# Six reorderings of products and banks in a one-core decoder trunk: up products, a w_out tile, embedding banks, triangular products, a branch tile, first masks

## The chip, the cores and the metric

The kernel runs on one core of one Trainium2 chip. The metric is the device time of one execution in microseconds (us), as a median of runs.

## The reference

One layer of a decoder trunk on a stream x of 512 tokens and 1024 channels, in fp32. The parts that the change touches:

```python
# mixer: one input projection gives q, k, v of three token mixers and three gates
proj = x @ w_in
(da_q, da_k, da_v, sb_q, sb_k, sb_v, dl_q, dl_k, dl_v, gates) = split(proj)
# A differential attention (4 heads), C dilated attention (12 heads), and
# B stick-breaking attention (8 heads):
z = q @ k.T * scale
log_keep = where(before, log_sigmoid(-z), 0.0)
later = cumsum(log_keep, axis=3, reverse=True) - log_keep
a = where(before, exp(log_sigmoid(z) + later), 0.0)
o = a @ v
# each branch: o_i @ w_branch_i;  merged = sum_i sigmoid(gate_i) * branch_i
x = layer_norm(alpha * x + merged @ w_out)
# MLP with squared ReLU, 1024 -> 4096 -> 1024, and a gated embedding of 256 channels
x = layer_norm(alpha * x + relu(x @ w_up)**2 @ w_down + sigmoid(x @ w_g) * (p @ w_p))
```

## The kernel before, in words

**Products.** Every product of fp32 matrices is three products of split operands (`mm3`, lines 86 to 89): a rounded high part and a low remainder, high by high (L87), high by low (L88), low by high (L89). Each writes a bank of PSUM, 128 x 512 fp32.

**Weights.** Weights come in chunks of 128 x 1024. The SyncE queue loads a chunk into one of six raw slots (L211, L213). ACT (ScalarE) casts it to the high part (L243, `wh<-raw`) and DVE (VectorE) subtracts to the low part (L245, `wl<-raw,wh`). The pair lies in a ring of six slots, and a slot is free again when PE (TensorE) has run the last product on the chunk six places earlier. Sums of weight chunks for the seven-product scheme below are made in DRAM by transfers that GpSimd (POOL) issues.

**Order.** `trunk()` fills a list `items`. An item has chunks `c`, the code that issues its products `mm`, the code that reads the bank out `ev`, the chunks that it needs, and the function that gives it a bank. A loop (L1970 to L2053) walks the list: it waits until the chunks are split, issues the reading out of the previous item, steps the side generators (stick-breaking heads `sb_head`, dilated heads, blocks of the differential attention `da_block`), and issues the item's products. A list scheduler then orders the instructions of each engine by its own estimates; each engine runs its list in that order.

**Banks.** PSUM has eight banks in two rotating pools: `mm_bank` (L80, two banks) and `at_bank` (L83, six). An item takes a bank from the pool of two if it names none.

**Up projection.** The MLP's up product is done in eight column groups, here called layers 0 to 7 after `up_parts(m)` (L1159). Each runs a seven-product scheme on 2 x 2 blocks: operand "12" of the weights against one form of x, "11" against another, and sums of blocks (operands 0, 1, 2) against t6, t7 and others. It is done for two pairs of column halves, j = 0 and 1; each pair keeps one bank `x` of the pool of two, whose left half (HB) and right half (HC) are 256 wide. `part_a(j)` does the "12"-product (12 products of 256 columns) into HC, ACT copies HC out (L1195), then the "11"-product (12 products) goes into HB of the same bank, and DVE adds the two (L1201). Parts b, c and e follow. The first layers stand alone; from layer 1 on, parts of the down projection are put between (`mlp_items`, L1310).

**The other places.** `wout_items` multiplies the merged branches, turned by PE (`turn_item`: transposes L794, ACT cast L798, DVE L799), by w_out (L887 to L889), eight steps k per tile of 128 tokens. `ple_items` multiplies the embedding by w_p (L955 to L960, copy L961). `first_branch` multiplies branch outputs by w_branch (L690 to L692), beside blocks of the differential attention, which turn rotary columns on DVE (L101). `t_item` makes transposed q and k tiles (mm3, then L101) and yields to the side generators once in its loop over k. `sb_head` sums log_keep over keys by products with a triangular matrix (`tri_r`, L1666) for four key blocks kb; blocks 3 and 2 share one bank of 512 columns, 256 each.

Of the kernel before, what the change touches and what calls it, by code (L numbers as in the profile page):

```python
# [55 lines left out]
def trunk(tc, a, out):  # L56
    nc = tc.nc
    es = ExitStack()
    with es:
# [14 lines left out]
        def slot(name, dt=F32):  # L74
            return big.tile([P, 512], dt, name=nm(name), tag="s", bufs=NSLOT)
# [190 lines left out]
        def item(cs, mm, ev, need=None, bank=None, size=1.0):  # L266
            items.append({"c": cs, "mm": mm, "ev": ev, "need": need, "bank": bank, "size": size})
# [24 lines left out]
        def t_item(nt, name, j):  # L292
            w = a["wt"][nt - 2]
            cs = [chunk(w.rearrange("p k m -> p (k m)"), 1024)]
            k0 = 1 if nt < 4 else 0

            def mm(ps):
                c = cs[0]
                for k in range(k0, 8):
                    s = slice(k * P, k * P + P)  # L300
                    mm3(ps, c["h"][:, s], c["l"][:, s], xh[k], xl[k], k == 0, k == 7)
                    if k == 3:
                        yield

            item(cs, mm, t_evac(name, j), bank=(lambda: begun[nt - 2]) if k0 else None)
# [55 lines left out]
        HB = slice(0, 256)  # L361
# [318 lines left out]
        def first_branch():  # L680
            for half in range(2):
                cs = [chunk(a["wb"][half, c].rearrange("p k n -> p (k n)"), 1024) for c in range(2)]
                for tt in range(4):
                    def mm(ps, tt=tt, cs=cs):
                        q = slice(tt * P, tt * P + P)
                        for k in range(4):
                            c = cs[k // 2]
                            n = slice(k % 2 * 512, k % 2 * 512 + 512)
                            h, lo = oTs[4 + k]
                            nc.tensor.matmul(ps, h[:, q], c["h"][:, n], start=k == 0, stop=False)  # L690
                            nc.tensor.matmul(ps, h[:, q], c["l"][:, n], start=False, stop=False)
                            nc.tensor.matmul(ps, lo[:, q], c["h"][:, n], start=False, stop=k == 3)  # L692

                    def ev(ps, tt=tt, half=half):
                        t = slot("b1")
                        e = nc.scalar.copy(t, ps)
                        marks.append(getattr(e, "ins", e))
                        merged[tt, half] = t
                    item(cs if tt == 3 else [], mm, ev, need=cs, size=0.5)
                    items[-1]["rate"] = 2.4  # L700

        bsum = {i: [dram.tile([P, 1024], F32, name=f"bsum{i}_{j}") for j in range(4)] for i in (0, 2)}
# [174 lines left out]
        def wout_items():  # L877
            for half in range(2):
                cs = [chunk(a["wo"][half, c].rearrange("p k n -> p (k n)"), 1024) for c in range(4)]
                for tt in range(4):  # L880
                    def mm(ps, tt=tt, cs=cs):
                        for k in range(8):
                            c = cs[k // 2]
                            s = slice((k % 2) * 512, (k % 2) * 512 + 512)
                            h, lo = merged_T[k // 4, tt // 2, k % 4 // 2]
                            q = slice(k % 2 * 256 + tt % 2 * P, k % 2 * 256 + tt % 2 * P + P)
                            nc.tensor.matmul(ps, h[:, q], c["h"][:, s], start=k == 0, stop=False)  # L887
                            nc.tensor.matmul(ps, h[:, q], c["l"][:, s], start=False, stop=False)
                            nc.tensor.matmul(ps, lo[:, q], c["h"][:, s], start=False, stop=k == 7)  # L889

                    def ev(ps, tt=tt, half=half):
                        y = xn.pop((tt, half))
                        if not half:
                            x1sum[tt] = small("lsm", 2)
                        i = nc.vector.scalar_tensor_tensor(y, y, ALPHA, ps, op0=OP.mult, op1=OP.add,
                                                           accum_out=x1sum[tt][:, half:half + 1])
                        st["added"] = getattr(i, "ins", i)
                        x1[tt, half] = y
                        if half:
                            pending.append(ln1_gen(tt))  # L900
                    item(cs if tt == 3 else [], mm, ev, need=cs, bank=at_bank)
                    for t in {0: [(1, 1, 0), (1, 1, 1)], 1: [(0, 1, 0), (0, 1, 1)]}.get(tt, ()) if not half else ():
                        turn_item(*t)
# [41 lines left out]
        def ple_items():  # L945
            cs = [chunk(a["wp"][half].rearrange("p k n -> p (k n)"), 1024) for half in range(2)]
            for half in range(2):
                for tt in range(4):
                    def mm(ps, tt=tt, half=half):
                        c = cs[half]  # L950
                        for k in range(2):
                            s = slice(k * 512, k * 512 + 512)
                            q = slice(tt * P, tt * P + P)
                            h, lo = pTs[k]
                            nc.tensor.matmul(ps, h[:, q], c["h"][:, s], start=k == 0, stop=False)  # L955
                            nc.tensor.matmul(ps, h[:, q], c["l"][:, s], start=False, stop=False)
                            nc.tensor.matmul(ps, lo[:, q], c["h"][:, s], start=False, stop=k == 1)

                    def ev(ps, tt=tt, half=half):
                        t = slot("ple")  # L960
                        nc.scalar.copy(t, ps)  # L961
                        ple[tt, half] = t
                    item([cs[half]] if tt == 3 else [], mm, ev, need=cs, bank=at_bank)


        sums_first = set()
# [192 lines left out]
        def up_parts(m):  # L1159

            cs = {}
            wu = a["wu"][m]

            def operand(n):
# [3 lines left out]

            def pair(j):
                js = slice(256 * j, 256 * j + 256)  # L1170
                b = {}

                def prod(ps, p, n, start, stop):
                    c = cs[n]
                    for k in range(4):
                        s = slice(512 * j + k * P, 512 * j + k * P + P)
                        mm3(ps, c["h"][:, s], c["l"][:, s], *forms[p][k], start and k == 0, stop and k == 3)
# [7 lines left out]
                def add(need, mm, ev, bank):  # L1185
                    if j == 0:
                        for n in need:
                            operand(n)
                    item([cs[n] for n in need] if j else [], mm, ev, need=[cs[n] for n in need], bank=bank)

                def part_a():
                    def mm(ps):
                        prod(ps[:, HC], 2, "12", True, True)
                        b["s"] = slot("up")
                        nc.scalar.copy(b["s"][:, HB], ps[:, HC])  # L1195
                        prod(ps[:, HB], 1, "11", True, False)

                    def ev(ps):
                        if j == 0:
                            hid[m] = [slot("hid") for _ in range(4)]  # L1200
                        nc.vector.tensor_add(hid[m][0][:, js], ps[:, HB], b["s"][:, HB])  # L1201
                    add(("12", "11"), mm, ev, bank("x", mm_bank))

                def part_b():
                    def mm(ps):
# [403 lines left out]
        def sb_head(hd):  # L1609
# [51 lines left out]
                yield  # L1661
            ah, al = {}, {}
            for kb, bi, c0, n in reversed(blk):
                ps = bank[bi][:, c0:c0 + n]
                for hl in (sph, spl):
                    nc.tensor.matmul(ps, tri_r, hl[bi][:, c0:c0 + n], start=False, stop=False, skip_group_check=True)  # L1666
                if kb < 3:
                    n2, hl = later[kb]
                    for t in hl:
                        nc.tensor.matmul(bank[bi][:, c0 + n - n2:c0 + n], ones_r, t, start=False, stop=False,  # L1670
                                         skip_group_check=True)
                if kb == 3:
                    continue
                n = w[bi]
                e = slot("a")[:, :n]
                nc.scalar.activation(e, bank[bi][:, :n], AF.Exp)
                h = slot("ah", F32R)[:, :n]
                lo = slot("al", F32R)[:, :n]
                nc.vector.tensor_copy(h, e)
                nc.vector.tensor_sub(lo, e, h.bitcast(F32))  # L1680
                ah[bi], al[bi] = h, lo
                if kb != 1:
                    yield
# [474 lines left out]
```

## Time and profile before

| | |
|---|---|
| runs shown | 1039.53, 1039.94, 1040.59 us; median 1039.94 |
| profiled execution | 1040.08 us, span 1038.1 us |
| granted clock of TensorE | 0.998 |
| PE busy | 1028.0 us (99%) |
| weight loads | 881.2 us (85%), beside PE |
| DVE busy | 787.0 us (76%) |
| ACT busy | 591.7 us (57%) |
| POOL busy | 180.1 us (17%) |

A row of the timeline has the start, the busy time, the engine, line and operation, and in brackets the engine's idle time just before it and what released it. PE's products are pipelined, so their busy times overlap; what one costs is read from the distance of its start to the next. PEld is the load of a product's stationary operand.

### The profile page before, as it was taken

The numbers are of one execution on the slowest core, as the hardware profiler recorded it, in microseconds if no ns is written. First come the engines' busy times: TensorE is split into PE (matmuls) and PEld (weight loads), VectorE is DVE, ScalarE is ACT, GpSimd is POOL, SyncE is SP. The second block draws the span as 40 slices with busy tenths as digits, with TensorE's granted clock in tenths as the row PEclk, the third lists the DMA queues.
The fourth block names the chain that finished last, engine by engine and source line by source line (L and its number), as shares of the span: only waits on it lengthen the run. The fifth ranks groups of instructions, "written<-read, shape, count | busy, mean of one in ns | idle before, by whom it ended". The sixth has DMA issues, their size and how long they took to land.

```text
span 1038.1 us, 15050 instructions
## 1 busy us (share of the span) xinstructions
PE 1028.0 (99%) x5448; PEld 881.2 (85%) x5448; DVE 787.0 (76%) x1412; ACT 591.7 (57%) x1010; POOL 180.1 (17%) x271
## 2 busy tenths in 40 slices
PE   9999999999999999999999999999999999999997
PEld 6888888889888888888888888889999889889886
DVE  6888667769765657779688885798768877877965
ACT  7566544536434645676675743775666556555651
POOL 0002411120211232411011040111111111111001
PEclk9999999999999999999999999999999999999999
DMA  8449968485976999977789795579999999998612
GB/s 309 121 156 271 277 193 217 120 290 144 285 182 222 271 272 294 238 205 199 227 269 235 267 320 182 160 222 319 331 290 315 301 306 340 303 295 279 235 57 81
DMA packets 71322, 249.21 MB, mean 240 GB/s; under 512 B 8808, under 2 KB 9592, under 8 KB 71248
## 3 DMA queue, kind: packets, MB, share of 16 engines
q0 software_dynamic: 32464, 116.21, 44.8%
q1 hardware_dynamic: 38208, 131.13, 35.1%
q8 instruction: 43, 0.70, 0.3%
q10 hardware_dynamic: 576, 0.92, 0.2%
q14 instruction: 31, 0.25, 0.1%
HBM read 246.10 MB, written 98.59 MB: 332 GB/s over the span
## 4 chain that ended last, share of the span: by engine, by line
PE 94%; DVE 2%; ACT 1%; DMA 1%; issue 1%; SPq 0%; POOL 0%; DVEq 0%; ACTq 0%; POOLq 0%
PE mm L87 10%; PE mm L88 10%; PE mm L89 10%; PE at L1261 4%; PE at L1262 4%; PE at L1263 4%; PE at L599 3%; PE at L600 3%; PE at L601 3%; PE mm L496 2%; PE mm L498 2%; PE mm L497 2%; PE at L89 1%; PE at L88 1%; PE at L87 1%; PE at L761 1%
## 5 line engine op out<-in xcount | busy, mean ns | idle before, releaser
L243 ACT CAST wh<-raw 128x1024 fp32r<-128x1024 f32 x257 | 268.6, 1049 | 242.0 <-PE mm L88 134.2
L245 DVE TENSOR_TENSOR wl<-raw,wh 128x1024 fp32r<-128x1024 f32 x257 | 312.7, 1223 | 112.9 <-ACT wh L243 111.3
L87 PE MATMUL mm<-xhT,wh 128*128 128x512 f32 x302 | 119.1, 394 | 0.0
L89 PE MATMUL mm<-xhT,wl 128*128 128x512 f32 x302 | 118.2, 391 | 0.0
L88 PE MATMUL mm<-xlT,wh 128*128 128x512 f32 x302 | 118.1, 391 | 0.0
L1261 PE MATMUL at<-wh,hh 128*128 128x512 f32 x188 | 73.7, 392 | 0.0
L87 PE MATMUL mm<-x1hT,wh 128*128 128x256 f32 x256 | 73.7, 288 | 0.0
L1262 PE MATMUL at<-wl,hh 128*128 128x512 f32 x188 | 73.7, 392 | 0.0
L1263 PE MATMUL at<-wh,hl 128*128 128x512 f32 x188 | 73.1, 389 | 0.0
L88 PE MATMUL mm<-x1lT,wh 128*128 128x256 f32 x256 | 72.2, 283 | 0.0
L89 PE MATMUL mm<-x1hT,wl 128*128 128x256 f32 x256 | 71.8, 283 | 0.0
L89 PEld LDWEIGHTS mm<-xhT,wl 128*128 128x128 f32 x302 | 56.8, 188 | 11.9
L87 PEld LDWEIGHTS mm<-xhT,wh 128*128 128x128 f32 x302 | 56.7, 188 | 11.0
L88 PEld LDWEIGHTS mm<-xlT,wh 128*128 128x128 f32 x302 | 56.7, 188 | 10.8
L87 PEld LDWEIGHTS mm<-x1hT,wh 128*128 128x128 f32 x256 | 48.7, 190 | 4.8 <-ACT up L1195 3.0
L88 PEld LDWEIGHTS mm<-x1lT,wh 128*128 128x128 f32 x256 | 48.8, 191 | 1.5
L89 PEld LDWEIGHTS mm<-x1hT,wl 128*128 128x128 f32 x256 | 48.6, 191 | 0.0
L1095 POOL DMA_DIRECT2D usum<-in_wu_dram x32 | 28.3, 921 | 101.6 <-DMA usum<-usum 34.8
L1095 POOL DMA_DIRECT2D dsum<-in_wd_dram x28 | 25.6, 936 | 102.5 <-DMA dsum<-dsum 37.0
L1263 PEld LDWEIGHTS at<-wh,hl 128*128 128x128 f32 x188 | 35.3, 188 | 7.7
L1261 PEld LDWEIGHTS at<-wh,hh 128*128 128x128 f32 x188 | 35.5, 189 | 6.0
L1262 PEld LDWEIGHTS at<-wl,hh 128*128 128x128 f32 x188 | 35.5, 189 | 5.5
(601 smaller groups left out, 2677.2 us busy)
## 6 DMA issues: line engine op xcount, KB each, us to landing
usum<-in_wu_dram POOLq DMA_DIRECT2D x48, 512.0 KB, 9.0
dsum<-in_wd_dram POOLq DMA_DIRECT2D x42, 512.0 KB, 8.9
raw<-in_wt_dram SPq DMA_DIRECT2D x38, 512.0 KB, 5.1
raw<-usum SPq DMA_DIRECT2D x32, 512.0 KB, 7.7
raw<-dsum SPq DMA_DIRECT2D x28, 512.0 KB, 7.0
raw<-in_wd_dram SPq DMA_DIRECT2D x25, 512.0 KB, 6.1
raw<-in_wu_dram SPq DMA_DIRECT2D x24, 512.0 KB, 7.6
raw<-in_wv_dram SPq DMA_DIRECT2D x18, 512.0 KB, 5.7
```

The source lines that it names most:

```text
L87: nc.tensor.matmul(ps, wh, xh, start=start, stop=False, skip_group_check=True)
L88: nc.tensor.matmul(ps, wh, xl, start=False, stop=False, skip_group_check=True)
L89: nc.tensor.matmul(ps, wl, xh, start=False, stop=stop, skip_group_check=True)
L243: i = nc.scalar.copy(h, raw)
L245: i = nc.vector.tensor_sub(lo, raw, h.bitcast(F32))
L599: nc.tensor.matmul(ps, h[:, q], c["h"][:, n], start=go, stop=False, skip_group_check=True)
L600: nc.tensor.matmul(ps, h[:, q], c["l"][:, n], start=False, stop=False, skip_group_check=True)
L601: nc.tensor.matmul(ps, lo[:, q], c["h"][:, n], start=False, stop=end, skip_group_check=True)
L1095: i = nc.gpsimd.dma_start(o, i, accum_op=OP.add, max_dma_last_dim=4096)
L1261: nc.tensor.matmul(ps, h[:, q], c["h"][:, s], start=go, stop=False, skip_group_check=True)
L1262: nc.tensor.matmul(ps, h[:, q], c["l"][:, s], start=False, stop=False, skip_group_check=True)
L1263: nc.tensor.matmul(ps, lo[:, q], c["h"][:, s], start=False, stop=end, skip_group_check=True)
```

## The change

1. Up products: `part_a(0)` does the "12"-products of both pairs, each into its own bank with its own copy; `part_a(1)` does the "11"-products of both, and issues pair 0's add (`first(0)`) between them. The chunk "11" is asked for with `part_a(1)`, so that in layers with down parts one down chunk is loaded ahead of it.
2. The third w_out tile (tt = 2, half 0) runs its steps k in the order 4 to 7, 0 to 3.
3. Embedding tiles 1 and 3 of half 0 take a bank of the pool of two.
4. For kb = 3 and 2 the triangular products of 256 columns become one of 512 for the high and one for the low part.
5. The branch tile tt = 1 of half 0 takes a bank of the pool of six.
6. `t_item` for nt = 2 yields after k = 4 instead of 3.

```diff
-                    if k == 3:
+                    if k == (4 if nt == 2 else 3):
                         yield
...
-                    item(cs if tt == 3 else [], mm, ev, need=cs, size=0.5)
+                    item(cs if tt == 3 else [], mm, ev, need=cs, size=0.5,
+                         bank=at_bank if tt == 1 and not half else None)
...
-                    def mm(ps, tt=tt, cs=cs):
-                        for k in range(8):
+                    ks = (4, 5, 6, 7, 0, 1, 2, 3) if tt == 2 and not half else range(8)
+
+                    def mm(ps, tt=tt, cs=cs, ks=ks):
+                        for k in ks:
...
-                    item([cs[half]] if tt == 3 else [], mm, ev, need=cs, bank=at_bank)
+                    item([cs[half]] if tt == 3 else [], mm, ev, need=cs,
+                         bank=None if tt % 2 and not half else at_bank)
...
                 def part_a():
+                    def first(i):
+                        nc.vector.tensor_add(hid[m][0][:, 256 * i:256 * i + 256], both[i]["x"][:, HB],
+                                             both[i]["s"][:, HB])
+
                     def mm(ps):
-                        prod(ps[:, HC], 2, "12", True, True)
-                        b["s"] = slot("up")
-                        nc.scalar.copy(b["s"][:, HB], ps[:, HC])
-                        prod(ps[:, HB], 1, "11", True, False)
+                        for i in range(2):
+                            if j == 0:
+                                if i:
+                                    both[i]["x"] = mm_bank()
+                                x, k = both[i]["x"], "12"
+                                prod(x[:, HC], 2, k, True, True, i)
+                                both[i]["s"] = slot("up")
+                                nc.scalar.copy(both[i]["s"][:, HB], x[:, HC])
+                            else:
+                                prod(both[i]["x"][:, HB], 1, "11", True, False, i)
+                                if not i:
+                                    first(i)
...
-                    add(("12", "11"), mm, ev, bank("x", mm_bank))
+                    operand(("12", "11")[j])
+                    need = [cs[("12", "11")[j]]]
+                    item(need, mm, ev, need=need, bank=(lambda: b["x"]) if j else bank("x", mm_bank))
...
-                ps = bank[bi][:, c0:c0 + n]
-                for hl in (sph, spl):
-                    nc.tensor.matmul(ps, tri_r, hl[bi][:, c0:c0 + n], start=False, stop=False, skip_group_check=True)
+                for hl in (sph, spl) if kb != 2 else ():
+                    nc.tensor.matmul(bank[bi][:, :w[bi]], tri_r, hl[bi], start=False, stop=False,
+                                     skip_group_check=True)
```

**Up products on PE, layer 0.** Before: the first product of each run of products, and the waits that it has. `mm_1497` is pair 0's bank, `mm_1503` pair 1's, `wh_1477` is chunk "12", `wh_1480` chunk "11", `wh_1483` and `wh_1486` the next operands; each run has 12 products but where the other pair cuts it in two (4 and 8, or 11 and 1).

```order
L87 MATMUL mm_1497_6921<-x1hT_6343,wh_1477_6820 128x256 [waits Activation_49]
...
L87 MATMUL mm_1503_6955<-x1hT_6343,wh_1477_6820 128x256
...
L87 MATMUL mm_1497_6921<-x1hT_6343,wh_1480_6826 128x256 [waits Activation_49]
...
L88 MATMUL mm_1503_6955<-x1lT_6344,wh_1477_6820 128x256
...
L89 MATMUL at_1511_6996<-t7h_1431_6602,wl_1484_6866 128x256 [waits DVE_49]
...
L87 MATMUL mm_1503_6955<-x1hT_6343,wh_1480_6826 128x256 [waits Activation_49]
...
L87 MATMUL mm_1497_6921<-t6h_1443_6642,wh_1486_6871 128x256 [waits DVE_49]
```

Now, with pair 1's bank named `mm_1499`:

```order
L87 MATMUL mm_1497_6905<-x1hT_6327,wh_1477_6804 128x256 [waits Activation_49]
...
L87 MATMUL mm_1499_6920<-x1hT_6327,wh_1477_6804 128x256
...
L87 MATMUL mm_1497_6905<-x1hT_6327,wh_1480_6810 128x256 [waits Activation_49]
...
L87 MATMUL mm_1499_6920<-x1hT_6327,wh_1480_6810 128x256 [waits Activation_49]
...
L89 MATMUL at_1511_6980<-t7h_1431_6586,wl_1484_6850 128x256 [waits DVE_49]
...
L87 MATMUL mm_1497_6905<-t6h_1443_6626,wh_1486_6855 128x256 [waits DVE_49]
```

Pair 0's "11"-product stood 4 products behind its "12"-product and now stands 12 behind; pair 1's stood 11 behind and now stands 12 behind.

**The copies on ACT, layer 0.** Before: the two copies of the "12"-products (L1195), and what stands around them.

```order
L1195 COPY up_1498_6934<-mm_1497_6921 128x256 [waits PE_49]
L243 CAST wh_1505_6982<-raw_1479_6824 128x1024 [waits DMAHW6_49,PE_49,Activation_49]
L1195 COPY up_1504_6968<-mm_1503_6955 128x256 [waits PE_49]
L243 CAST wh_1508_6988<-raw_1482_6830 128x1024 [waits DMAHW7_49,PE_49,Activation_49]
L1211 COPY up_1498_6934<-at_1511_6996 128x256 [waits DVE_49,PE_49]
```

Now (the copies are on line 1209):

```order
L1209 COPY up_1498_6918<-mm_1497_6905 128x256 [waits PE_49]
L243 CAST wh_1501_6935<-raw_1479_6808 128x1024 [waits DMAHW6_49,PE_49,Activation_49]
L1209 COPY up_1500_6933<-mm_1499_6920 128x256 [waits PE_49]
L243 CAST wh_1508_6972<-raw_1482_6814 128x1024 [waits DMAHW7_49,PE_49,Activation_49]
L1253 ACTIVATE hid_1504_6941<-hid_1504_6941 128x512 [waits DVE_49]
```

A cast stands between the two copies in both. It takes the ring slot of the chunk six places back, which is `wh_1477`, chunk "12", in both; the same holds in the other layers.

**The embedding on PE.** Before: the first products of the embedding's tiles 1 to 3 of half 0, all in banks of the pool of six.

```order
L955 MATMUL at_1389_6448<-wh_1349_6217,pTh_1356_6255 128x512 [waits DVE_49,Activation_49]
...
L957 MATMUL at_1389_6448<-wh_1349_6217,pTl_1359_6260 128x512
L955 MATMUL at_1397_6469<-wh_1349_6217,pTh_1356_6255 128x512 [waits DVE_49,Activation_49]
...
L957 MATMUL at_1397_6469<-wh_1349_6217,pTl_1359_6260 128x512
L955 MATMUL at_1405_6490<-wh_1349_6217,pTh_1356_6255 128x512 [waits DVE_49]
```

Now:

```order
L958 MATMUL mm_1389_6432<-wh_1349_6201,pTh_1356_6239 128x512 [waits PE_49]
...
L960 MATMUL mm_1389_6432<-wh_1349_6201,pTl_1359_6240 128x512
L958 MATMUL at_1397_6453<-wh_1349_6201,pTh_1356_6239 128x512 [waits DVE_49,Activation_49]
...
L960 MATMUL at_1397_6453<-wh_1349_6201,pTl_1359_6240 128x512
L958 MATMUL mm_1405_6474<-wh_1349_6201,pTh_1356_6239 128x512
```

The order of the products is the same; tiles 1 and 3 no longer use up a bank of the pool of six, so the tiles behind them take banks that come two places earlier in its rotation.

More of the change, by code (lines that the diff above doesn't have):

```diff
@@ L886, in mm @@
                             q = slice(k % 2 * 256 + tt % 2 * P, k % 2 * 256 + tt % 2 * P + P)
-                            nc.tensor.matmul(ps, h[:, q], c["h"][:, s], start=k == 0, stop=False)
+                            nc.tensor.matmul(ps, h[:, q], c["h"][:, s], start=k == ks[0], stop=False)
                             nc.tensor.matmul(ps, h[:, q], c["l"][:, s], start=False, stop=False)
-                            nc.tensor.matmul(ps, lo[:, q], c["h"][:, s], start=False, stop=k == 7)
+                            nc.tensor.matmul(ps, lo[:, q], c["h"][:, s], start=False, stop=k == ks[-1])
                     def ev(ps, tt=tt, half=half):
@@ L1161, in up_parts @@
             cs = {}
+            both = [{}, {}]
             wu = a["wu"][m]
@@ L1170, in pair, with prod @@
                 js = slice(256 * j, 256 * j + 256)
-                b = {}
-                def prod(ps, p, n, start, stop):
+                b = both[j]
+                def prod(ps, p, n, start, stop, j=j):
                     c = cs[n]
@@ L1200, in ev @@
                             hid[m] = [slot("hid") for _ in range(4)]
-                        nc.vector.tensor_add(hid[m][0][:, js], ps[:, HB], b["s"][:, HB])
-                    add(("12", "11"), mm, ev, bank("x", mm_bank))
+                        else:
+                            first(1)
+                    operand(("12", "11")[j])
+                    need = [cs[("12", "11")[j]]]
+                    item(need, mm, ev, need=need, bank=(lambda: b["x"]) if j else bank("x", mm_bank))
                 def part_b():
```

## The prediction

> **What bounds the kernel now.** I read the page first, then the waits of the matrix engine, then the timeline around each place that the change touches.
>
> From the page: the span, the matrix engine's busy time, the transfers by slice, and the chain that ended last.
>
> ```profile
> span 1038.1 us, 15050 instructions
> PE 1028.0 (99%) x5448; PEld 881.2 (85%) x5448; DVE 787.0 (76%) x1412; ACT 591.7 (57%) x1010; POOL 180.1 (17%) x271
> ...
> DMA  8449968485976999977789795579999999998612
> ...
> PE 94%; DVE 2%; ACT 1%; DMA 1%; issue 1%; SPq 0%; POOL 0%; DVEq 0%; ACTq 0%; POOLq 0%
> ```
>
> PE is busy 99% and carries 94% of the chain. Nothing can be gained except products or PE's own waits. The change removes 16 products and otherwise reorders, so its worth is the waits it takes away less the waits it makes. The weight loads (PEld) show them, with total us, times and longest:
>
> ```profile
> PEld mm L87 <- ACT up L1195: 3.0, 13, 0.3
> ...
> PEld mm L690 <- PE at L147: 0.7, 1, 0.7
> PEld at L955 <- ACT ple L961: 0.6, 1, 0.6
> ...
> PEld at L887 <- ACT mh L798: 0.5, 1, 0.5
> ```
>
> Four of the six edits stand in this list: the up copies (13 waits), the branch tile (L690), the embedding (L955) and the w_out tile (L887).
>
> **Up products: the first copy.** Layer 0 on PE and ACT:
>
> ```profile
> 709.69 0.39 PE L1017 MATMUL at<-wh,x1hT 128*128 128x512 f32 x1
> 709.92 0.39 PE L1018 MATMUL at<-wl,x1hT 128*128 128x512 f32 x1
> ...
> 712.17 0.70 PE L87 MATMUL mm<-x1hT,wh 128*128 128x256 f32 x2
> 712.70 0.28 PE L88 MATMUL mm<-x1lT,wh 128*128 128x256 f32 x1
> ...
> 714.73 0.28 PE L88 MATMUL mm<-x1lT,wh 128*128 128x256 f32 x1
> 714.85 0.28 PE L89 MATMUL mm<-x1hT,wl 128*128 128x256 f32 x1
> ...
> 716.17 0.28 PE L88 MATMUL at<-t7l,wh 128*128 128x256 f32 x1
> 716.46 0.39 PE L87 MATMUL mm<-x1hT,wh 128*128 128x256 f32 x1
> 716.68 0.28 PE L88 MATMUL mm<-x1lT,wh 128*128 128x256 f32 x1
> ...
> 712.06 0.36 ACT L1195 COPY up<-mm 128x256 f32<-128x256 f32 x1
> ...
> 715.09 1.05 ACT L243 CAST wh<-raw 128x1024 fp32r<-128x1024 f32 x1 [2.67 <-issue]
> 716.04 0.37 ACT L1195 COPY up<-mm 128x256 f32<-128x256 f32 x1
> ```
>
> A 256-wide product starts 0.12 us after the one before (714.73, 714.85), a 512-wide one 0.23. From 712.17 two steps take 0.53 instead of 0.24, so the first copy costs 0.29: PE had only 4 products of the other pair for cover. Half is the wait, the other 0.10 the next step, whose weight load wasn't ahead. In layer 2 the place is milder:
>
> ```profile
> 766.93 0.39 PE L1263 MATMUL at<-wh,hl 128*128 128x512 f32 x1
> 767.22 0.38 PE L87 MATMUL mm<-x1hT,wh 128*128 128x256 f32 x1
> 767.44 0.28 PE L88 MATMUL mm<-x1lT,wh 128*128 128x256 f32 x1
> ```
>
> Here it is 0.06 (0.29 against 0.23) and 0.10. Eight layers lie between: 8 x 0.16 = 1.3 us, which I take; 8 x 0.29 = 2.3 would be the upper end, though the row of 3.0 for all 13 waits leaves 1.8 beside the second places below. After the change 12 products (1.44 us) stand between. In layer 0 the last product that the first copy waits for started four steps ahead of 712.17, at 711.69; thirteen steps on is 713.25, and the copy ended at 712.42, so it would be 0.8 early: **−1.3**.
>
> **Up products: the second copy.** It is not the same case. In the order, ACT has a weight cast between the two copies of each layer, before and after, and the cast waits for the ring slot of chunk "12", which PE frees with the last 12-product, the very product that the second copy waits for. Layer 0 shows what that makes: last product starts 714.85, cast 715.09, copy 716.04, and PE goes on at 716.46, 1.61 us after 714.85. With 11 products for cover it wanted to go on at 716.29: 0.17, and 0.10 in the next step. Layer 1 has the same with the cast released by PE:
>
> ```profile
> 735.81 1.05 ACT L243 CAST wh<-raw 128x1024 fp32r<-128x1024 f32 x1 [1.73 <-PE mm L88]
> 736.77 0.37 ACT L1195 COPY up<-mm 128x256 f32<-128x256 f32 x1
> ...
> 736.93 0.28 PE L88 MATMUL at<-t7l,wh 128*128 128x256 f32 x1
> 737.19 0.38 PE L87 MATMUL mm<-x1hT,wh 128*128 128x256 f32 x1
> ```
>
> 0.14 and 0.10. Layers 0, 1, 3, 5 and 7 have it, together 0.27 + 4 x 0.24 = 1.23. After the change the cast still stands ahead of the copy, and 12 products cover instead of 11. One product more is 0.12: it leaves 0.05 in layer 0, 0.02 in the others, and the 0.10 each, 0.63 in all: **−0.6**. In layers 2, 4 and 6 a down chunk's 6 or 12 products also stand between; no wait there. If the copy passed the cast, all 1.23 would go; that is the upper end, and zero the lower.
>
> [...]
>
> New waits here: the first add is now issued between the two 11-products, and the 6-product of its bank follows 24 products (2.9 us) later instead of 36. On the vector engine a split (L245) of the delayed cast stands ahead of it, so it ends about 2.9 us after 714.85's counterpart; the 6-product wants the bank 36 steps, 4.4 us, after it. Cover remains: 0. The chunk "11" is loaded after a down chunk in layers with downs; see the rivals.
>
> **Branch, w_out, embedding.**
>
> ```profile
> 426.30 0.69 DVE L101 SCALAR_TENSOR_TENSOR da_klb<-mm,da_kb 64x512 fp32r<-64x512 f32 x1
> ...
> 427.14 0.47 PE L690 MATMUL mm<-wh,oTh 128*128 128x512 f32 x1 [0.32 <-DVE da_klb L101]
> ...
> 619.05 0.59 ACT L798 CAST mh<-mm 128x512 fp32r<-128x512 f32 x1 [1.24 <-PE mm L794]
> ...
> 624.47 0.50 PE L887 MATMUL at<-wh,mh 128*128 128x512 f32 x1 [0.24 <-ACT mh L798]
> ...
> 664.28 0.56 ACT L961 COPY ple<-at 128x512 f32<-128x512 f32 x1
> ...
> 664.90 0.50 PE L955 MATMUL at<-wh,pTh 128*128 128x512 f32 x1 [0.21 <-ACT ple L961]
> ```
>
> The branch tile waits for a pool-of-two bank that L101 reads until 426.99. In the pool of six it gets a bank free long before; the later tiles shift by one bank, still free in time. It lies between 0.32 (PE idle) and 0.7 (PEld): **−0.5**. The w_out tile waits for halves that were turned just ahead; the order now puts 12 products on halves cast at 619.05 first, 12 x 0.23 = 2.7 us of cover. Between 0.24 and 0.5, plus the next step: **−0.5**. The embedding tile waits for a bank whose copy ran 664.28 to 664.84; with two tiles in the pool of two it takes one emptied earlier. Between 0.21 and 0.6: **−0.5**.
>
> **Triangular products.** 32 products of 256 become 16 of 512 (the first row counts half of them, the high ones):
>
> ```profile
> L1666 PE MATMUL at<-sph,tri_r x32: 278/310/398, 29.9 to 217.9; 128*128 128x256 f32 x16, 128*128 128x384 f32 x8, 128*128 128x512 f32 x8
> ```
>
> 2 x 0.12 − 0.23 = 0.01 each: **−0.2**, between 0 and 0.3. [...]
>
> **First masks.**
>
> ```profile
> 20.26 0.69 DVE L101 SCALAR_TENSOR_TENSOR sb_k<-at,sb_k 64x512 fp32r<-64x512 f32 x1
> ...
> 21.09 0.53 PE L146 MATMUL at<-sb_q,sb_k 128*128 128x256 f32 x2 [0.36 <-ACT wh L243]
> ...
> 30.49 0.69 DVE L101 SCALAR_TENSOR_TENSOR sb_qlb<-mm,sb_qb 64x512 fp32r<-64x512 f32 x1
> ...
> 31.33 0.47 PE L496 MATMUL mm<-wh,xhT 128*128 128x512 f32 x1
> ```
>
> Three products (0.68) go ahead of the masks and hide their 0.36. But at 31.33 PE waits for a bank that L101 reads until 31.18, at the end of a row of vector and scalar work that PE doesn't drive. PE comes there earlier and waits longer: **0**, at best −0.5.
>
> **Sum.** 1.3 + 0.6 + 0.5 + 0.5 + 0.5 + 0.2 = 3.6 us. The profiled execution took 1040.08 us (2.0 outside its span), 0.14 above the median of 1039.94. 1039.94 − 3.6 = 1036.3; I write 1036.4. A difference of 0.2%, 2.1 us, is about what a measurement of this kernel can tell from none.
>
> **Rivals.**
>
> 1. Everything pays: the second copies too (0.6), the masks (0.5) and the first copies up to 1.8 (0.5): −5.2, 1034.7. Against it: the cast's place in the order. Chance 0.10.
> 2. Part comes back: the three single waits (1.5) were standing in for the chains of layer norm and gates behind them, and PE waits there instead: −2.1, 1037.8; with half of Up −1.2, 1038.7. For it: the masks are such a case. Against: no wait of PE on layer norm is in the list. Chance 0.28, of which 0.16 is still below the 0.2%, 0.12 within it.
> 3. Slower: a late chunk. From 712 us on the transfers are at 0.9 or more, and a down chunk is now loaded ahead of "11". If a cast between the copies waits for its data, the second copy stands behind it, and PE behind that: per layer one microsecond for each that the chunk is late, beyond the slack. The slack is what casts now wait for PE:
>
> ```profile
> ACT wh L243 <- PE mm L88: 70.6, 26, 4.1
> ```
>
> 2.7 us in the mean. It decides where a chunk comes over 2.7 us later than now; one more microsecond in eight layers gives 8 − 3.6 = +4.4, 1044.3. Chance 0.10.
>
> **Numbers.** The forecast has 0.52. Faster by over 0.2%: 0.52 + 0.10 + 0.16 = 0.78; within: 0.12; slower: 0.10. The range takes in the bounds of the terms and the second rival, 1034.9 to 1038.7; what it leaves out is mostly the third.
>
> **What the next profile would show.** Right: the row of L87 on the up copy falls from 13 waits to five of about 0.1; the rows of L690, L955 and L887 vanish from the list; the wait at 31.33 grows by about 0.5. Wrong: PE waiting for a cast or for data in the up layers, second places with more than 0.2 each, or a new wait on layer norm after the embedding.

## The result and the profile after

The changed kernel took 1037.52 us in the median of 9 runs (1036.55 to 1038.24), beside 1040.39 of the kernel before (9 runs, 1039.53 to 1040.92). The ratio is 0.9973, with a 95% interval of 0.9964 to 0.9982: 2.8 us faster by that ratio, where 3.6 were forecast. The profiled execution took 1037.48 us.

The page of the changed kernel:

```profile
span 1035.5 us, 15013 instructions
PE 1025.9 (99%) x5432; PEld 880.2 (85%) x5432; DVE 786.4 (76%) x1412; ACT 592.9 (57%) x1010; POOL 180.5 (17%) x271
...
DMA  8349968495976999977889896479999999999512
...
PE 91%; issue 4%; DVE 2%; DMA 1%; ACT 1%; POOL 0%; DVEq 0%; POOLq 0%; ACTq 0%
```

PE has 16 products fewer and is as full as before. The waits of the weight loads, from the same list as before:

```profile
PEld at L762 <- DVE b L773: 0.7, 2, 0.5
...
PEld mm L496 <- issue: 0.6, 1, 0.6
...
PEld at L1709 <- DVE sb_v L509: 0.4, 1, 0.4
...
PEld at L1021 <- ACT x1r L940: 0.2, 1, 0.2
```

All four rows that the forecast spoke of (the up copies, L690, L955, L887) are gone; what is left at the up copies is too short for the list and shows on the timeline. So is the masks' own row (L146 behind a cast, 0.5). In its place L496 has come, the wait at 31 us that was forecast for the masks. L1709 and L1021 are new, and L762 had one wait of 0.2 before (then L761); these three were not forecast. (Rows of L347, behind `wh` and `wl`, which also differ, 1.0 and 0.2 before and 1.2 and 0.8 now, belong to the first 31 us, where PE waits for its first chunks.) The timeline of PE at the places of the forecast, in the order up copy of layer 1, branch, w_out, embedding, masks:

```profile
734.63 0.28 PE L89 MATMUL mm<-x1hT,wl 128*128 128x256 f32 x1
734.76 0.38 PE L87 MATMUL mm<-x1hT,wh 128*128 128x256 f32 x1
734.98 0.28 PE L88 MATMUL mm<-x1lT,wh 128*128 128x256 f32 x1
...
427.00 0.39 PE L147 MATMUL at<-da_klb,da_qb 128*128 128x512 f32 x1
427.23 0.39 PE L690 MATMUL at<-wh,oTh 128*128 128x512 f32 x1
...
624.40 0.48 PE L890 MATMUL at<-wh,mh 128*128 128x512 f32 x1
624.71 0.40 PE L891 MATMUL at<-wl,mh 128*128 128x512 f32 x1
...
664.17 0.39 PE L960 MATMUL mm<-wh,pTl 128*128 128x512 f32 x1
664.39 0.39 PE L958 MATMUL at<-wh,pTh 128*128 128x512 f32 x1
...
31.37 0.47 PE L496 MATMUL mm<-wh,xhT 128*128 128x512 f32 x1 [0.41 <-DVE sb_qlb L101]
```

The branch and the embedding tile start one step (0.23 or 0.22) after the product before them. The w_out tile keeps 0.08 (0.31 to the next start instead of 0.23) of the 0.55 that the waiting product and the step behind it had before. The up copy keeps what the cast ahead of it leaves: 0.13 to 734.76 and 0.22 to 734.98, so 0.01 of waiting and 0.10 in the next step. ACT shows the cast and the copy of that place in the order that the forecast had read:

```profile
733.39 1.05 ACT L243 CAST wh<-raw 128x1024 fp32r<-128x1024 f32 x1
734.34 0.37 ACT L1209 COPY up<-mm 128x256 f32<-128x256 f32 x1
```

The masks' gain is back at 31.37, where PE now idles 0.41. The three waits that were not forecast, and what stands ahead of the last on ACT:

```profile
61.84 0.39 PE L88 MATMUL mm<-xlT,wh 128*128 128x512 f32 x1
62.24 0.38 PE L1709 MATMUL at<-ah,sb_v 128*128 128x256 f32 x1
62.46 0.28 PE L1711 MATMUL at<-al,sb_v 128*64 128x256 f32 x1
...
555.01 0.39 PE L600 MATMUL at<-wl,xhT 128*128 128x512 f32 x1
555.52 0.50 PE L762 MATMUL at<-wh,oTh 128*128 128x512 f32 x1
555.86 0.39 PE L763 MATMUL at<-wl,oTh 128*128 128x512 f32 x1
...
671.31 0.49 PE L927 MATMUL at<-ident,xn 128*128 128x128 f32 x3
671.80 0.50 PE L1021 MATMUL at<-wh,x1hT 128*128 128x512 f32 x1
672.14 0.39 PE L1022 MATMUL at<-wl,x1hT 128*128 128x512 f32 x1
...
671.10 0.65 ACT L940 COPY x1r<-at 128x256 f32<-128x256 f32 x2 [0.66 <-DVE x1lT L934]
```

Against undisturbed steps they cost 0.27 (62 us), 0.39 (555 us) and 0.27 (672 us, of which 0.09 was there before).

### The profile page after: what moved, and what is told of

Same layout as the page of the kernel before. It is cut to its first block, busy times and chain, and to the rows that moved or that the text cites. A ratio compares the mean times of both kernels' runs of the same rounds, so it can differ in the third digit from the quotient of the medians.

```text
span 1035.5 us, 15013 instructions
## 1 busy us (share of the span) xinstructions
PE 1025.9 (99%) x5432; PEld 880.2 (85%) x5432; DVE 786.4 (76%) x1412; ACT 592.9 (57%) x1010; POOL 180.5 (17%) x271
## 4 chain that ended last, share of the span: by engine, by line
PE 91%; issue 4%; DVE 2%; DMA 1%; ACT 1%; POOL 0%; DVEq 0%; POOLq 0%; ACTq 0%
PE mm L87 10%; PE mm L89 10%; PE mm L88 10%; PE at L1281 4%; PE at L1282 4%; PE at L1283 4%; PE mm L496 2%; PE mm L498 2%; PE mm L497 2%; PE at L601 2%; PE at L599 2%; PE at L600 2%; PE at L89 1%; PE at L88 1%; PE at L87 1%
## 5 line engine op out<-in xcount | busy, mean ns | idle before, releaser
L245 DVE TENSOR_TENSOR wl<-raw,wh 128x1024 fp32r<-128x1024 f32 x257 | 312.4, 1222 | 115.8 <-ACT wh L243 114.4
L87 PE MATMUL mm<-xhT,wh 128*128 128x512 f32 x302 | 119.1, 395 | 0.0
L87 PE MATMUL mm<-x1hT,wh 128*128 128x256 f32 x256 | 72.8, 284 | 0.0
L87 PEld LDWEIGHTS mm<-xhT,wh 128*128 128x128 f32 x302 | 56.7, 188 | 11.3 <-PE mm L498 0.2
L87 PEld LDWEIGHTS mm<-x1hT,wh 128*128 128x128 f32 x256 | 48.9, 191 | 1.9
```

Of the source, the lines that this page charges most:

```text
L87: nc.tensor.matmul(ps, wh, xh, start=start, stop=False, skip_group_check=True)
L245: i = nc.vector.tensor_sub(lo, raw, h.bitcast(F32))
```

## The experiments

Eight kernels were timed, five to eleven runs each, in five rounds beside runs of the kernel before. Where the text says "excess", it is the distance between two starts of PE less the usual one for that width, read from the timeline. "Pace" is the mean step from one product of 512 columns to the next of that width between 95 and 250 us, over the steps of 0.20 to 0.26 us. The "lead" of a run is how much earlier PE starts the same product than in the kernel before.

**Up products alone.** Edit 1 on the kernel before, nothing else (the whole edit stands in the change above).

```diff
 def part_a():
+    def first(i):
...
     def mm(ps):
-        prod(ps[:, HC], 2, "12", True, True)
...
+        for i in range(2):
...
```

> Edit 1 alone. Theory: the up stage gives what the trace of the whole change shows there, 13 waits on the up copy going to five steps of 0.10, about -1.9 to -2.0 us, and nothing is given back before or behind it, so the time is 1.9 us below before (ratio 0.9981). Rival: PE that is earlier in the up stage waits for casts or data later, so that the whole change's 2.8 us come mostly from the other edits: then this gives under 1 us.

Measured: 1037.67 us, ratio 0.9976 (0.9966 to 0.9986). PE leads by 0.27 us when the up stage begins (710 us) and by 2.48 at the end: the stage gives 2.2 us. The 0.27 is left of a lead of 0.4 from the first 31 us, where chunks arrive at other times from run to run (the casts that end ACT's first two waits for a DMA start at 4.39 and 6.64 us in before, at 4.22 and 7.03 in the change). The theory holds, at 2.2 rather than 1.9 us; the rival falls.

**Everything but the up products.**

Against the change (`up_parts` as before, edits 2 to 6 in place):

```diff
-                        for i in range(2):
-                            if j == 0:
...
+                        prod(ps[:, HC], 2, "12", True, True)
+                        b["s"] = slot("up")
+                        nc.scalar.copy(b["s"][:, HB], ps[:, HC])
+                        prod(ps[:, HB], 1, "11", True, False)
```

> Edits 2 to 6 without the up products. Theory: the branch's 0.5 is spent in a wait of about 0.4 near 555 us where PE waits for a bank whose reading stands behind a split of a chunk that comes late from DRAM, the masks' gain is spent at 31.3 us, and a wait of 0.27 near 62 us is new; what is left is w_out and the embedding, 0.9 less 0.3 at 672 us, so -0.6 to -0.9 us (ratio 0.9992). Rival: the waits at 62, 555 and 672 us are scatter of one execution; then -1.7 us (ratio 0.9984).

Measured: 1039.04 us, ratio 0.9989 (0.9980 to 0.9998). The five edits together give 1.1 us where the forecast had 1.7. The waits are there again: 0.25 at 61.8 us, 0.59 at 555 us, 0.27 at 671.7 us. In the profiled execution, one of the slower of the eleven (1039.70), PE's lead is 0.4 at 40 us and 0.4 at the end: there the gains and the waits cancel. The time (a gain of 0.2 to 2.1) does not tell the theory from its rival; the waits, there again, do. Of them the one at 555 us differs most between executions.

**The change a second time.** The same kernel, for a second profile and a second timing.

> The change as it is, a second profile. Theory: the waits at 62 us (0.27), 555 us (0.39) and 671.8 us (0.27) are there again within 0.1 each, and PE's start-to-start excess in the up stage is five times 0.10; time 2.8 us below before. Rival (scatter): at least two of the three differ by more than 0.2.

Measured: 1036.89 us, ratio 0.9967 (0.9955 to 0.9980). The waits at 62 us (0.26) and 672 us (0.26) are the same to 0.01. The one at 555 us is not there at all. The reading of PE's bank (L773, on DVE) stands behind the split of a chunk (L245), and the split waits for the cast of that chunk, which waits for its data from DRAM. Here the cast and the split in the change's first profile, then the cast in this one, where the split starts at 552.43 and waits for nothing:

```profile
551.96 1.05 ACT L243 CAST wh<-raw 128x1024 fp32r<-128x1024 f32 x1 [4.15 <-DMA raw<-in_wgm_dram]
553.04 1.23 DVE L245 TENSOR_TENSOR wl<-raw,wh 128x1024 fp32r<-128x1024 f32 x1 [0.42 <-ACT wh L243]
```

```profile
549.66 1.05 ACT L243 CAST wh<-raw 128x1024 fp32r<-128x1024 f32 x1 [1.96 <-DMA raw<-in_wgm_dram]
```

The same chunk, from the same place in the queue, came 2.3 us apart in two executions of one kernel. In the kernel before it came at 551.53 and PE just did not wait. So the wait at 555 us is scatter of a load that PE meets without slack; the other two belong to the kernel. It is not rare: of the six profiles with the branch edit four have it (0.30 to 0.59), of the six without it one (0.13). That the 0.5 us of the edit makes the difference is not shown: PE was due there at 555.24 in the change and at 555.27 in before. The theory holds for two of three.

**The second up copies on the vector engine.** Against the change:

```diff
-                                nc.scalar.copy(both[i]["s"][:, HB], x[:, HC])
+                                (nc.vector.tensor_copy if i else nc.scalar.copy)(both[i]["s"][:, HB], x[:, HC])
```

> The change, with the second copy of each layer made by the vector engine, where it stands ahead of the split of the chunk whose cast stands ahead of it on ACT. Theory (the cast ahead of the copy makes what is left): the five steps of 0.10 in layers 0, 1, 3, 5 and 7 vanish, 0.5 us faster than the change. Rival (what is left is the price of any first product on a bank that another engine has read, or the vector engine is as late): the five stay, time equal to the change within 0.2 us.

Measured: 1036.57 us, ratio 0.9969 (0.9957 to 0.9980), not to be told apart from the change by time (one of its six runs took 1040.02). By the profile, layer 1 has no step left, and the copy runs ahead of the split:

```profile
732.83 0.42 DVE L1209 COPY up<-mm 128x256 f32<-128x256 f32 x1 [0.24 <-PE mm L89]
733.79 1.23 DVE L245 TENSOR_TENSOR wl<-raw,wh 128x1024 fp32r<-128x1024 f32 x1 [0.54 <-ACT wh L243]
...
734.31 0.28 PE L89 MATMUL mm<-x1hT,wl 128*128 128x256 f32 x1
734.43 0.28 PE L87 MATMUL mm<-x1hT,wh 128*128 128x256 f32 x1
734.55 0.28 PE L88 MATMUL mm<-x1lT,wh 128*128 128x256 f32 x1
```

Layers 1, 3, 5 and 7 lose their 0.10; layer 0 gets 0.27 instead of 0.16, since there the copy stands behind other work of the vector engine (L991 from 712.63, the copy at 713.23). Net 0.3 us, not 0.5. That the cast ahead of the copy makes what was left is shown for four of five layers.

**First masks alone.** On the kernel before:

```diff
-                    if k == 3:
+                    if k == (4 if nt == 2 else 3):
```

> Edit 6 alone. Theory: its 0.5 us at 21 us come back in full as a wait of 0.56 at 31.3 us, and it makes the wait of 0.27 at 62 us; so 0.0 to +0.3 us against before (ratio 1.0000 to 1.0003). If also the pace of 512-wide products between 95 and 250 us is its doing, that reads 229.4 ns there instead of 228.8 (546 of them, +0.3 us), and the sum is +0.6. Rival: the wait at 62 us comes from the merged triangular products; then neither shows here.

Measured: 1040.20 us, ratio 1.0002 (0.9993 to 1.0011). No wait at 62 us, and the pace is 228.7 ns (538 steps), as before. The gain comes back ten microseconds later:

```profile
32.15 0.47 PE L496 MATMUL mm<-wh,xhT 128*128 128x512 f32 x1 [0.44 <-DVE sb_qlb L101]
```

So edit 6 is worth nothing, and the wait at 62 us is not its doing: the rival holds.

**Triangular products alone.** On the kernel before:

```diff
-                for hl in (sph, spl):
-                    nc.tensor.matmul(ps, tri_r, hl[bi][:, c0:c0 + n], start=False, stop=False, skip_group_check=True)
+                for hl in (sph, spl) if kb != 2 else ():
+                    nc.tensor.matmul(bank[bi][:, :w[bi]], tri_r, hl[bi], start=False, stop=False,
+                                     skip_group_check=True)
```

> Edit 4 alone. Theory: a pair of 256-wide products takes 236 ns there and one of 512 takes 233, so the 16 merges save 0.05 to 0.1 us in all, not 0.2; ratio 0.9999. If the slower pace of the other 512-wide products between 95 and 250 us (229.4 against 228.8 ns) comes with it, it costs 0.3 and the sum is +0.2 us. Rival: the pace is that of the masks' shift; then it reads 228.8 here.

Measured: 1040.72 us, ratio 1.0005 (0.9997 to 1.0014). The time alone does not settle the sign. The profile has the wait at 61.8 us (0.24) and the slower pace, 229.3 ns (547 steps). The merges themselves save 0.07 us per ten (between 95 and 260 us 20 products of 256 took 2.37 us in before, and ten of 512 take 2.30 in the change's second profile). So by the profile edit 4 costs 0.24 + 0.3 − 0.1, near +0.45 us; PE's lead falls from 0.41 at 40 us to nothing by 200 us.

**The four other edits.**

Against the change (edits 1, 2, 3 and 5 in place):

```diff
-                    if k == (4 if nt == 2 else 3):
+                    if k == 3:
...
-                for hl in (sph, spl) if kb != 2 else ():
+                for hl in (sph, spl):
```

> Edits 1, 2, 3 and 5, without masks and triangular products. Theory: no wait at 62 us, the pace between 95 and 250 us at 228.8 ns, the other gains as in the whole change, so 0.5 us faster than the change: 3.3 us below before (ratio 0.9968). Rival: those two edits carry their own weight; then this is equal to the change or slower by 0.2.

Measured: 1036.77 us, ratio 0.9965 (0.9953 to 0.9977). No wait at 62 us, pace 228.7 ns, span 1034.8 us beside 1035.5 and 1035.0 of the change. The mechanism is as the theory has it; by time it is not told apart from the change (0.9973 and 0.9967).

**The four, with copies of layers 1 to 7 on the vector engine.**

```diff
+                                (nc.vector.tensor_copy if i and m else nc.scalar.copy)(both[i]["s"][:, HB],
+                                                                                       x[:, HC])
```

> As the last, and with the second up copy of layers 1 to 7 on the vector engine. Theory: the 0.10 steps of layers 1, 3, 5 and 7 go as in the run with all second copies there, and layer 0 keeps its 0.10 instead of the 0.27 that it had there; so 0.4 us faster than the last (ratio 0.9964). Rival: what the vector engine's copy displaces there comes back as a wait; then no faster.

Measured: 1036.15 us, ratio 0.9961 (0.9949 to 0.9974), the fastest median of all, 3.9 us below before, though its interval overlaps those of the last and of the change. Layer 0 keeps its 0.16 and the other layers have none, as expected.

**Merged in heads 0 and 1 alone.** On the kernel before (an excerpt):

```diff
+                wide = hd < 2
+                cols = slice(0, w[bi]) if wide else slice(c0, c0 + n)
+                for hl in (sph, spl) if kb != 2 or not wide else ():
...
```

> Merged triangular products in heads 0 and 1 alone (4 merges of 16). These two move the order: on ACT a weight cast goes eight places forward, and on PE the first products of a later head's output go 13 forward. Theory (the order costs, not the merge): the wait of 0.24 to 0.27 at 62 us is there, and it alone or with the slower pace of 512-wide products between 95 and 250 us (229.4 ns). Rival (the merge itself slows the products beside it): pace 228.8 there, since no head after 70 us is merged.

**Merged in heads 2 to 7 alone.** The same, but for one line:

```diff
+                wide = hd >= 2
```

> Merged triangular products in heads 2 to 7 alone (12 of 16), which leaves the order at 62 us as before. Theory (the order costs): no wait at 62 us, and pace 228.8 between 95 and 250 us, so PE gains about 12 times 6 ns there. Rival (the merge itself slows the products beside it): no wait at 62 us, pace 229.4.

Both were profiled and run once: 1040.00 and 1040.02 us beside 1040.19 of before. The profiles split the two costs. With heads 0 and 1 merged the wait at 62 us is there (0.26) and the pace is 228.8; with heads 2 to 7 merged the wait is not there and the pace is 229.3. PE at 61 us in the first and in the second:

```profile
61.27 0.39 PE L88 MATMUL mm<-xlT,wh 128*128 128x512 f32 x1
61.66 0.39 PE L1691 MATMUL at<-ah,sb_v 128*128 128x256 f32 x1
```

```profile
60.95 0.40 PE L89 MATMUL mm<-xhT,wl 128*128 128x512 f32 x1
61.18 0.28 PE L1691 MATMUL at<-ah,sb_v 128*128 128x256 f32 x1
```

So the wait is the order's. With heads 0 and 1 merged the list scheduler puts four weight casts on ACT one or two places forward, the first two each ahead of a copy of `sb_v` (the expectation read this as one cast eight places forward). The vector engine's work behind them runs later, at its end the last subtraction for `sb_v` (L509), which starts at 61.18 instead of 61.00 and ends at 61.60, where PE wants it at 61.50. The pace comes with the merges of the later heads, so in that point the rival holds. Where it sits: behind the merged products and two of `ones_r`, PE is slower for ten products. From the kernel before, and then with heads 2 to 7 merged:

```profile
114.75 0.28 PE L1670 MATMUL at<-sph,ones_r 128*128 128x256 f32 x1
114.87 0.28 PE L1670 MATMUL at<-spl,ones_r 128*128 128x256 f32 x1
114.98 0.40 PE L87 MATMUL mm<-xhT,wh 128*128 128x512 f32 x1
...
117.26 0.39 PE L88 MATMUL mm<-xlT,wh 128*128 128x512 f32 x1
```

```profile
114.29 0.28 PE L1672 MATMUL at<-sph,ones_r 128*128 128x256 f32 x1
114.41 0.28 PE L1672 MATMUL at<-spl,ones_r 128*128 128x256 f32 x1
114.52 0.40 PE L87 MATMUL mm<-xhT,wh 128*128 128x512 f32 x1
...
116.85 0.39 PE L88 MATMUL mm<-xlT,wh 128*128 128x512 f32 x1
```

Ten steps from the first L87 take 2.28 us before and 2.33 after a merge, and so behind all five merges between 110 and 215 us. But slow steps are not the merge's alone. In the kernel before, ten steps behind products of 384 and 256 columns take 2.33 us too:

```profile
38.27 0.28 PE L1670 MATMUL at<-smp,ones_r 128*128 128x256 f32 x1
38.38 0.40 PE L496 MATMUL mm<-wh,xhT 128*128 128x512 f32 x1
...
40.72 0.39 PE L497 MATMUL mm<-wl,xhT 128*128 128x512 f32 x1
```

At 62 us ten steps take 2.31 in the kernel before, behind four triangular products of 256 columns, and 2.28 with heads 2 to 7 merged, where the order of the products there is the same as before. So neither the width of the triangular products nor the order alone fixes how long the ten steps take. What makes them slower the rows do not show; that stays open.

## Why the prediction was right, and where its terms were off

The sign and most of the mechanism were right; the sum was 0.8 us too large. By the time alone the forecast is not set apart from its second rival: 2.8 lies about midway between 3.6 and 2.1. The traces do that, term by term, and two terms were off in opposite directions:

- **Up products, −1.9 forecast: −2.2 measured** alone, from 710 us to the end. The second copies left what was forecast: five steps of 0.10, in layers 0, 1, 3, 5 and 7 and nowhere else, with 0.06 of waiting in layer 0 and 0.01 in the others, 0.63 in all. Reading the cast between the copies in the order, and its release by the very product that the copy waits for, was what made this term: with the copy on the other engine the steps of 0.10 went in four of the five layers. What the waits were before was misread. The place in layer 2 from which the forecast took 0.16 for each first copy is the second copy's:

```profile
762.15 0.35 ACT L1195 COPY up<-mm 128x256 f32<-128x256 f32 x1
766.80 0.37 ACT L1195 COPY up<-mm 128x256 f32<-128x256 f32 x1
...
762.42 0.40 PE L1262 MATMUL at<-wl,hh 128*128 128x512 f32 x1
762.66 0.28 PE L87 MATMUL mm<-x1hT,wh 128*128 128x256 f32 x1
```

The first copy ends at 762.50, and PE goes on at 762.66 without excess; the excess at 767.22 follows the second, which ends at 767.17. So "no wait there" was wrong for the second copies of layers 2, 4 and 6, which had 0.16 to 0.17 each. By the steps, the first copies cost 1.17 in seven layers and lost it all, near the 1.3 by luck, and the second fell from 1.73 to 0.63, by 1.1 instead of 0.6. That the list's 13 waits looked like eight first and five second copies was luck too: the steps show an excess at 15 copies.

- **Branch, −0.5: −0.5 at its place.** What was left out is that PE meets a load without slack at 555 us, which took back 0.4 in the change's first profile and nothing in the second. There, too, PE waits for a chain behind the place, as the second rival had it, but only where the chunk is late.
- **w_out, −0.5: −0.5.** Of 0.55, 0.08 stays in the step behind its first product.
- **Embedding, −0.5: −0.3.** The wait went, but PE then met the layer norm's chain at 671.8 us: the copy of x1's parts on ACT that ended at 671.75. The forecast had named such a wait as a sign of being wrong. This is the second rival's mechanism, here in every profile with the edit. It was set at nothing because no such wait stood in the list of before; the list shows waits, and a chain with no wait can still have none to spare.
- **Triangular products, −0.2: near +0.45.** The step that failed. The 0.01 per merge was taken from rounded rows; it measured 0.007. More important, only the products were priced. The removal of products moved casts on ACT in the order (0.25), and the products behind five of the merges ran slower (0.3). The first could have been looked for in ACT's order at 62 us before the run; the second only by comparing the steps behind blocks of other widths, which in before take 2.28 (at 114.98 us) to 2.33 us (at 38.38) for ten.
- **Masks, 0: 0.** The wait of 0.4 that PE had at 21 us stands at 31.4 us in the change and at 32.15 in the run of the masks alone.

2.2 + 0.5 + 0.5 + 0.3 − 0.45 is 3.05. From 40 us to the end PE gains 3.1 us on before in the change's second profile and 2.6 in the first, which has the 0.39 at 555 us. The times say 2.8 and, in the second timing, 3.4 (ratio 0.9967); they also hold the first 31 us, where PE waits for its first chunks and the executions lie up to 0.8 us from that of before.

The third rival, a late chunk in the up stage, did not come: in the change's two profiles PE has no excess there beyond the six steps of 0.10 (five at second copies, one that was there before) and the waiting of 0.06 in layer 0.

## What to carry to other kernels

When a wait is covered with more work, look in the order for what stands ahead of its releaser on that engine, and what releases that: here a copy behind a cast was as late as the cast (in the change the cast started at 733.39 and the copy behind it at 734.34), and what will be left of the wait can be read off before the run. Match each wait with its releaser in the timeline before pricing it; a count that fits the list is no proof. An edit that removes a few instructions in a kernel ordered by a scheduler has two prices, that of the instructions and that of the new order, and the second can be the larger (by the profiles the merges saved 0.1 us, and the order took 0.25 at 62 us); compare the order on the engines that the edit does not touch. A gain at one place is worth no more than the slack of the next chain that PE meets, and a chain without a wait in the list may have none (the layer norm's at 672 us took back 0.18 of the embedding's 0.5).

## What the runs showed of the hardware that was not expected

Products of 512 columns do not start at their usual pace behind some blocks of other products: at 38.38 us in before the first step took 0.241 us and the eleventh 0.227. Ten steps took 2.33 us behind two merged triangular products and two of 256 columns (114.52 us with heads 2 to 7 merged), and 2.28 behind six of 256 columns at the same place (114.98 us in before). The pace was 229.3 to 229.4 ns in all six profiles with heads 2 to 7 merged and 228.7 to 228.8 in all six without. Why is open. One load of a weight chunk landed 2.3 us apart in two executions of the same kernel (the cast that waited for it started at 551.96 and at 549.66 us), and PE lost 0.39 us at 555 us in the first and nothing in the second.
